# A two-layer trunk on one core: gate projections moved beside the block inverses, background blocks held back during one, and their weights loaded one call ahead

## The chip, the cores and the metric

The kernel runs on one core of a Trainium2 chip. The metric is the device time of one execution in microseconds (us). Each kernel is run several times and the median counts. One further execution is profiled; all durations below come from it.

The core has a matrix engine (PE, with its weight loads shown apart as PEld), a vector engine (DVE), an activation engine (ACT), a general engine (POOL) and a queue engine (SP) that issues most DMA transfers. Each engine takes its instructions strictly in the order of the program, and waits with everything behind it when one is not ready.

## The reference

A trunk of two layers over 1024 tokens of 1024 features. Layer 0 mixes the tokens by a gated delta net, layer 1 by retention; both are followed by a convolutional feed-forward network. Six vectors per layer (shift, scale and gate of mixer and network) come from a conditioning vector `e` and a large matrix `ada_w`. Cut to what matters here:

```python
def gated_deltanet(h, w_in, conv_w, a_log, dt_bias, norm_w, w_out):   # 8 heads of 128, chunks of 64
    qkv, z, a, bt = jnp.split(h @ w_in, ...)
    qkv = jax.nn.silu(causal_dwconv(qkv, conv_w))
    ...
    sol = lax.linalg.triangular_solve(kk + eye, rhs, left_side=True, lower=True, unit_diagonal=True)
    ...
    _, o = lax.scan(step, state0, xs)
    o = o * lax.rsqrt(jnp.mean(o * o, axis=-1, keepdims=True) + 1e-6) * norm_w
    o = o * jax.nn.silu(z)
    return o.reshape(...) @ w_out

def reference(...):
    e = jax.nn.silu(c @ cond_w + cond_b)
    for i in range(DEPTH):
        mod = (e @ ada_w[i] + ada_b[i])[:, None, :]
        sh1, sc1, g1, sh2, sc2, g2 = jnp.split(mod, 6, axis=-1)
        y = mixers[i % N_MIXERS](x * (1.0 + sc1) + sh1)
        x = layer_norm(DN_ALPHA * x + (1.0 + g1) * y, ln_g[i, 0], ln_b[i, 0])
        y = conv_ffn(x * (1.0 + sc2) + sh2, ...)
        x = layer_norm(DN_ALPHA * x + (1.0 + g2) * y, ln_g[i, 1], ln_b[i, 1])
```

## The kernel before

**Arithmetic.** All products are single precision, made of three products of a high and a low part each (`mm3`: low by high, high by low, high by high). A weight block of 128x1024 is loaded into a buffer `wr` (`load_w`, L102), ACT copies it to the high part `wh` (L89) and DVE subtracts to get the low part `wl` (L90). `wr`, `wh` and `wl` have two buffers each: a load starts when the split of the block two before has ended. All these loads are issued by SP, in program order.

**The delta-net phase** (about 87 to 658 us of the span) is written as streams: Python generators that issue instructions and name the next time on a hand-kept clock (`run`, table `LAT`) at which they want to go on. `run` always takes the stream that is ready and has the lowest number. The order that PE gets in this phase is pinned to the order of issue (`pq`, under L636 and L639); the other engines' orders are made by a list scheduler, which may move an instruction ahead of others of its engine. The streams are:

- `filler`: the projections, as items. An item "c" is one block of 128 features of q, k or v for all tokens: 48 matmuls of 128x512, then the causal convolution (`conv_half`), eight rows of DVE at L457. An item "z" is one block of the gate projection (weights `gdn_wz`): 48 matmuls as well, then SiLU on ACT (L1084) and a store to scratch memory `zd` (L1085). The items in the list `items` are all "c"; a "z" is put in by `filler` where a "c" would wait for a `qkv` buffer, and the rest of the eight at the end.
- `t_front(p)`: decays and key products of a pair of heads.
- `t_solve(0)` and `t_solve(1)`: for four heads each, the inverses of all 32x32 triangular blocks by forward substitution on DVE: a transpose X to Y (L797), 31 steps of a multiply (L805) and a subtract (L807), and transposes RX (L811) and TX (L815) of the result; ACT copies between them.
- `t_chain(p)`: builds the inverses of 64x64 and 128x128 from these on PE, beginning with 64 matmuls of 32x32.
- `prep(p)`, `dt_half(p, h)` (DT, L953), `scan(p, half)` (u, L976; Sn, L989) and a tail: products for the scan, the scan over chunks and its normalisation.

After the phase, `gate_phase` reads the gates back from `zd` (zg, L1116), multiplies them with the normalised output (L1129), and the output projection with `gdn_wout` (L303 to L305) follows, first for one half of the tokens, then for the other.

**Background blocks.** The vectors that are needed later are made in small units: `bg_ada` appends to the list `bg` eight units for each vector. A unit loads 512 KB of `ada_w` into a `wr` buffer (tile `mvw`, L210) and adds two rows of blocks to an accumulator on DVE (L214, L216); the last unit of each half also uses PE and ACT (L226 to L230). `filler` runs one unit after every item (`bg_step`), so a unit's load is issued right before the rows that use it. Three vectors (24 units) are made in this phase. Other units run in the feed-forward and retention phases, from `strassen` and other places, there with tiles of the tag `lane` where `bg_tag` says so.

**At the start** the first half's transposed input blocks 0 to 3 are held in two tiles of the tag `xT`, blocks 4 to 7 in `wr` buffers (`hold`).

## Time and profile before

| what | value |
|---|---|
| median of 3 runs | 3033.51 us (3031.15 to 3038.18) |
| the profiled execution | 3032.61 us, of which its span 3030.8 us |
| mean granted PE clock | 0.971 |
| memory traffic | 450.22 MB, mean 149 GB/s |
| weight loads for the feed-forward network | 96 of 512 KB, landing 4.0 us after issue (median) |
| loads of `ada_w` | 80 of 512 KB |

The span is the time from the first to the last recorded instruction; the execution's own time is 1.8 us longer. A row of a groups view reads: line, engine, operation, output<-input by the program's names, shape, count, then busy us, mean ns of one, idle time of the engine just before, and what ended most of it. A timeline row begins with the start and the duration in us. A row of waits gives engine, tile and line, the engine waited for with its tile and line, and us, times, longest.

The page's picture of the whole span, in 40 slices of about 76 us with the busy share in tenths:

```profile
PE   8889998999999999998999999999999899999997
DVE  5785786545888888998788645566688887778988
ACT  4655555434544445445432442222243544445442
```

The delta-net phase is the second to the ninth digit of a row. The prediction shows the further lines.

### The profile page before, as it was taken

How to read it: one execution, taken by the hardware profiler on the slowest of the kernel's cores; microseconds unless marked ns; L12 is line 12 of the kernel's file. 1: busy time of each engine (PE TensorE's matmuls, PEld its weight loads, DVE VectorE, ACT ScalarE, POOL GpSimd, SP SyncE). 2: the span in 40 equal slices, each digit the busy share in tenths (PEclk: the TensorE clock that was granted, in tenths of full speed). 3: DMA queues.
4: the chain of work that ended last, by engine and by line, in shares of the span. 5: the costliest groups of instructions: out<-in, count | busy, mean ns of one | idle time of the engine just before them, and what ended most of it. 6: DMA issues, size and time to landing. Idle time of an engine off the chain costs nothing. (4 is left out here: it accounts for less than half of the span.)

```text
span 3030.8 us, 38796 instructions
## 1 busy us (share of the span) xinstructions
PE 2840.2 (94%) x13590; PEld 2312.4 (76%) x13590; DVE 2271.4 (75%) x3841; ACT 1316.8 (43%) x2408; POOL 672.8 (22%) x629
## 2 busy tenths in 40 slices
PE   8889998999999999998999999999999899999997
PEld 7768876887778788786777787767777678888785
DVE  5785786545888888998788645566688887778988
ACT  4655555434544445445432442222243544445442
POOL 0410311033021111730023303422200011113704
PEclk9999998999999999999999999999998999999998
DMA  7222221354344545854322444666663332336663
GB/s 271 89 70 74 98 82 62 116 170 138 106 153 151 158 158 182 309 193 141 126 105 98 166 160 144 200 184 186 202 217 132 98 136 104 105 105 227 232 188 108
DMA packets 243027, 450.22 MB, mean 149 GB/s; under 512 B 22928, under 2 KB 76432, under 8 KB 242832
## 3 DMA queue, kind: packets, MB, share of 16 engines
q1 hardware_dynamic: 211648, 400.02, 40.0%
q10 hardware_dynamic: 29760, 43.00, 3.9%
q0 software_dynamic: 1424, 4.72, 0.4%
q8 instruction: 107, 1.75, 0.2%
q14 instruction: 88, 0.72, 0.1%
HBM read 339.13 MB, written 108.53 MB: 148 GB/s over the span
## 5 line engine op out<-in xcount | busy, mean ns | idle before, releaser
L636 PE MATMUL acc<-hT,wh 128*128 128x512 f32 x960 | 302.8, 397 | 0.0
L1556 POOL TENSOR_TENSOR o<-o 128x512 f32<-128x512 f32 x88 | 121.1, 1386 | 725.4 <-DVE o L1549 622.9
L279 PE MATMUL acc<-bb,ab 128*128 128x512 f32 x504 | 205.5, 408 | 18.8 <-DVE bb L90 18.7
L1158 PE MATMUL acc<-T,wb 128*128 128x512 f32 x840 | 205.3, 393 | 8.7 <-DVE wb L90 8.6
L636 PEld LDWEIGHTS acc<-hT,wh 128*128 128x128 f32 x960 | 184.3, 192 | 34.5
L278 PE MATMUL acc<-bb,ab 128*128 128x512 f32 x504 | 192.2, 407 | 16.9 <-DVE ab L90 10.3
L636 PE MATMUL acc<-hT,wl 128*128 128x512 f32 x480 | 204.3, 426 | 0.3 <-ACT sg L1084 0.3
L89 ACT ACTIVATE ab<-ar 128x512 fp32r<-128x512 f32 x210 | 129.8, 624 | 168.6 <-PE acc L280 87.9
L280 PE MATMUL acc<-bb,ab 128*128 128x512 f32 x504 | 202.6, 403 | 0.0
L1158 PEld LDWEIGHTS acc<-T,wb 128*128 128x128 f32 x840 | 157.9, 189 | 46.1 <-DVE wb L90 12.4
L90 DVE TENSOR_TENSOR wb<-wr,wb 128x512 fp32r<-128x512 f32 x162 | 116.0, 718 | 92.8 <-ACT wb L89 89.5
L90 DVE TENSOR_TENSOR ab<-ar,ab 128x512 fp32r<-128x512 f32 x210 | 169.2, 812 | 15.1 <-ACT ab L89 14.7
L90 DVE TENSOR_TENSOR wl<-wr,wh 128x1024 fp32r<-128x1024 f32 x85 | 106.4, 1252 | 89.7 <-ACT wh L89 89.7
L90 DVE TENSOR_TENSOR wb<-mm,wb 128x512 fp32r<-128x512 f32 x216 | 145.1, 683 | 22.8 <-ACT wb L89 20.9
L89 ACT ACTIVATE wh<-wr 128x1024 fp32r<-128x1024 f32 x101 | 106.8, 1058 | 121.3 <-PE acc L636 56.1
L89 ACT ACTIVATE wb<-mm 128x512 fp32r<-128x512 f32 x216 | 122.8, 593 | 72.5 <-DVE mm L1204 72.4
L1215 ACT ACTIVATE pc<-acc 128x512 f32<-128x512 f32 x143 | 84.5, 593 | 154.0 <-PE acc L1158 95.2
L636 PE MATMUL acc<-wh,hT 128*128 128x512 f32 x384 | 138.0, 422 | 2.0 <-DVE vv L90 2.0
L89 ACT ACTIVATE wb<-wr 128x512 fp32r<-128x512 f32 x162 | 99.3, 627 | 92.2 <-DMA wr<-in_ffn_up 45.9
L1535 DVE SCALAR_TENSOR_TENSOR o<-g,vc,o 128x512 f32<-128x512 f32 (+2 forms) x176 | 138.2, 804 | 0.8 <-ACT o L1530 0.2
L457 DVE SCALAR_TENSOR_TENSOR qkv<-raw,vc,qkv 128x512 f32<-128x512 f32 x144 | 114.6, 800 | 30.4 <-ACT qkv L455 29.3
L279 PEld LDWEIGHTS acc<-bb,ab 128*128 128x128 f32 x504 | 98.9, 196 | 44.7 <-DVE bb L90 24.3
(634 smaller groups left out, 7792.0 us busy)
## 6 DMA issues: line engine op xcount, KB each, us to landing
wr<-in_ffn_up SPq DMA_DIRECT2D x96, 512.0 KB, 4.0
mvw<-in_ada_w SPq DMA_DIRECT2D x80, 512.0 KB, 4.3
ad<-o SPq DMA_DIRECT2D x154, 256.0 KB, 2.2
ar<-ad SPq DMA_DIRECT2D x154, 256.0 KB, 4.4
Br<-in_ffn_down SPq DMA_DIRECT2D x88, 256.0 KB, 4.1
wr<-in_ret_wv SPq DMA_DIRECT2D x32, 512.0 KB, 3.7
ar<-od SPq DMA_DIRECT2D x56, 256.0 KB, 5.3
xs<-xt ACTq DMA_DIRECT2D x24, 512.0 KB, 3.8
```

The lines of the kernel that those rows point to most:

```text
L89: act.activation(dst_h, src, AF.Copy)
L90: eng.tensor_tensor(dst_l, src, dst_h, ALU.subtract)
L278: mm(acc, a[1][:, sl], w[0], start=first, stop=False)
L279: mm(acc, a[0][:, sl], w[1], start=False, stop=False)
L280: mm(acc, a[0][:, sl], w[0], start=False, stop=last)
L457: dve.scalar_tensor_tensor(oh, raw[:, 3 - j:515 - j], w[:, 3 - j:4 - j], oh, ALU.mult, ALU.add)
L636: pq(pe.matmul(out, lhsT, rhs, start=start, stop=stop), cost)
L1158: return pe.matmul(*a, skip_group_check=True, **kw)
L1215: act.activation(t, X, AF.Copy)
L1535: dve.scalar_tensor_tensor(tv, gv[:, c0 - j:c1 - j], w[:, 2 - j:3 - j], tv, ALU.mult, ALU.add)
L1556: pool.tensor_tensor(o[d], o[x], o[y], op)
```

## The change

It has five parts.

1. The order of the items is fixed. z 0, 1 and 2 follow the item (c, 0), in the place where solve 0 runs; z 3 follows the last k item (c, K + 7); z 4 to 7 come at the end. Before, `filler` placed the first two at a later point and six at the end.
2. A flag `quiet` is set when `t_solve` takes its tile X and cleared when it has issued TX; `filler` runs no background unit while it is set.
3. A background entry is now a pair of a fetch and a unit. `bg_step` issues the fetch of the next entry before it runs the current unit; `bg_flush`, at the start and the end of `strassen`, runs a unit whose fetch is out without fetching a further one.
4. `wr` has three buffers. For it the tag `xT` goes: blocks 0 to 3 of the first half are held in tiles of the tag `cv`.
5. The three vectors of this phase are made in the order 2, 4, 3, not 4, 3, 2.

The diff, shortened:

```diff
...
     dr = ctx.enter_context(tc.tile_pool(name="dr", bufs=1, space=bass.MemoryType.DRAM))
 
     BUFS = {"hTa": 8, "hTb": 8, "qkv": 24, "aux": 4, "auh": 8, "lane": 4, "cv": 4, "ada": 1,
-            "wr": 2, "wh": 2, "wl": 2, "t2": 3, "sm": 14, "sm2": 6, "st": 8, "s8": 6, "S": 4, "qx": 3, "fs": 1, "xT": 2}
+            "wr": 3, "wh": 2, "wl": 2, "t2": 3, "sm": 14, "sm2": 6, "st": 8, "s8": 6, "S": 4, "qx": 3, "fs": 1}
 
     def tl(tag, shape, dt=F32, name=None):
         return sb.tile(shape, dt, tag=tag, name=name or tag, bufs=BUFS[tag])
...
     bg_ps = [None]
     bg_tag = ["wr"]
 
-    def bg_step(tile=mm_tile):
+    def bg_step(tile=mm_tile, ahead=True):
         bg_ps[0] = tile
         if bg:
-            bg.pop(0)()
+            unit = bg.pop(0)[1]
+            if ahead and bg and bg[0][0]:
+                bg[0][0]()
+                bg_ahead[0] = True
+            else:
+                bg_ahead[0] = False
+            unit()
+
+    bg_ahead = [False]
+
+    def bg_flush():
+        if bg_ahead[0]:
+            bg_step(ahead=False)
 
     def gemm_feat(src, hT_, step=True):
         w = load_w(src)
...
     def bg_ada(i, j, kind):
         box = {}
 
+        def fetch(nh, kp):
+            wr = box[nh, kp] = tl(bg_tag[0], [P, 2, HALF], name="mvw")
+            c0 = j * D + nh * HALF
+            sp.dma_start(wr, A["ada_w"][i, kp * 256:(kp + 1) * 256, c0:c0 + HALF].rearrange("(a p) n -> p a n", p=P))
+
         def unit(nh, kp):
             if kp == 0:
                 box["a"] = tl("ada", [P, HALF])
             a = box["a"]
-            wr = tl(bg_tag[0], [P, 2, HALF], name="mvw")
-            c0 = j * D + nh * HALF
-            sp.dma_start(wr, A["ada_w"][i, kp * 256:(kp + 1) * 256, c0:c0 + HALF].rearrange("(a p) n -> p a n", p=P))
+            if (nh, kp) not in box:
+                fetch(nh, kp)
+            wr = box.pop((nh, kp))
             for kk in range(2):
                 k = kp * 2 + kk
                 if k == 0:
...
 
         for nh in range(2):
             for kp in range(KT // 2):
-                bg.append(lambda nh=nh, kp=kp: unit(nh, kp))
+                bg.append((lambda nh=nh, kp=kp: fetch(nh, kp), lambda nh=nh, kp=kp: unit(nh, kp)))
 
     def fold(i, which, ln_idx):
         sh, sc = vecs[i, 3 * which], vecs[i, 1 + 3 * which]
...
 
         for c in range(2):
             for r in range(8):
-                bg.append(lambda c=c, r=r: unit(c, r))
+                bg.append((None, lambda c=c, r=r: unit(c, r)))
 
     def ln_hooks(half, xts, tag, vecs2, out, dst, key, npool=0):
         def build(f):
...
                     xT["w"] = tl("wr", [P, 2, HALF], name="xT")
                 t = xT["w"][:, f % 2]
             else:
-                t = tl("auh" if half else "xT", [P, HALF], name="xT")
+                t = tl("auh", [P, HALF], name="xT") if half else tl("cv", [P, 516], name="xT")[:, 0:HALF]
             act.activation(t, turn(half, f), AF.Copy)
             xT[half, f] = t
 
...
         yield after_ev(("T0", 2 * qd_ - 1), ("A", 2 * qd_), ("A", 2 * qd_ + 1))
         yield from take("lane", 1)
         X = tl("lane", [P, 32, 32], name="X")
+        quiet[0] = True
         for h in pairs[2 * qd_] + pairs[2 * qd_ + 1]:
             for b in range(4):
                 bs = slice(32 * b, 32 * b + 32)
...
         TX = tl("lane", [P, 32, 32], name="TX")
         dve.transpose(flat(TX), flat(TP))
         RTX[qd_] = (RX, TX)
+        quiet[0] = False
         give("lane", 1)
         emit(("Tq", qd_))
         emit(("T", qd_), LAT["T"])
...
             give("lane", 1)
             emit(("M", p))
 
-    bg_ada(0, 4, "col")
-    bg_ada(0, 3, "col")
-    bg_ada(0, 2, "col")
+    for j in (2, 4, 3):
+        bg_ada(0, j, "col")
     kept = {}
     zd = dr.tile([GH, P, S], F32, tag="zd", name="zd")
 
...
         ssq_tile(ti, ptr)
         emit(("f", ti), 1.0)
 
+    quiet = [False]
+
     def filler(items):
-        spare = [(z, k) for k in range(GH)]
-        todo = list(items)
-        while todo or spare:
-            if not todo or (todo[0][0] == "c" and free["qkv"] < 2 and len(spare) > 4):
-                kind, ti = spare.pop(0)
-            else:
-                kind, ti = todo.pop(0)
+        for kind, ti in items:
             if kind == "h":
                 if ti > 1:
                     acc = acc_tile()
...
                     yield [(0.2, ssq_late(ti))]
                 else:
                     emit(("f", ti), LAT["fv"])
-            bg_step(acc_tile)
+            if not quiet[0]:
+                bg_step(acc_tile)
 
     LAT = {"kk": 3.05, "ld": 1.14, "g1": 17.30, "gm": 2.50, "mm": 1.81, "T": 4.98, "X": 3.38, "fs": 1.9, "T0": 5.00, "t1": 1.65, "t2": 2.35, "t3": 1.34, "D": 2.67, "s1": 1.60, "s2": 1.22, "s3": 1.26, "tail": 12.31, "ssq": 9.30, "fv": 2.85}
     pairs = [(2 * p, 2 * p + 1) for p in range(GH // 2)]
...
     events["Sh", -1] = events["Sh", -2] = 0.0
     c, z = "c", "z"
     K, V = GH, 2 * GH
-    items = [("h", 1), ("h", 2), ("h", 3), (c, K + 3), (c, V), (c, V + 1), (c, 0), (c, 1), (c, V + 2), (c, V + 3), (c, 2), (c, 3),
-             (c, K + 4), (c, K + 5), (c, K + 6), (c, K + 7), (c, V + 4), (c, V + 5), (c, 4), (c, 5), (c, V + 6), (c, V + 7), (c, 6), (c, 7)]
+    items = ([("h", 1), ("h", 2), ("h", 3), (c, K + 3), (c, V), (c, V + 1), (c, 0), (z, 0), (z, 1), (z, 2)]
+             + [(c, k) for k in (1, V + 2, V + 3, 2, 3, K + 4, K + 5, K + 6, K + 7)]
+             + [(z, 3), (c, V + 4), (c, V + 5), (c, 4), (c, 5), (c, V + 6), (c, V + 7), (c, 6), (c, 7), (z, 4), (z, 5), (z, 6), (z, 7)])
     todo = [(-1.0, gates()), (9.0, filler(items))]
     todo += [(0.3, t_solve(0)), (2.3, t_solve(1))]
     for p in range(4):
...
         return b
 
     def strassen(hT0, xts, scale, shift, items, tags=("hTb", "hTb", "qkv", "qkv", "aux"), direct=False):
+        bg_flush()
         B = {"11": hT0[:4], "21": hT0[4:]}
         nblk = [0]
         nacc = [0]
...
             wino(n, items[n][2]())
             if items[n][3]:
                 items[n][3]()
+        bg_flush()
         bg_tag[0] = "wr"
         return B
 
```

What moves on the engines, at three places. Line numbers of the changed kernel are up to 19 higher than those before: L805 and L807 (the solve's steps) are L823 and L825, L457 (convolution) is L474, L216 (background) is L233, L210 (its load) is L219.

DVE, in the middle of solve 0, before the change (fs and T are the solve's own, the number of elements rising and falling with the step):

```order
L805 TENSOR_TENSOR fs_1464<-Y_1459,T_1461 128x240
L457 SCALAR_TENSOR_TENSOR qkv_1658<-raw_1659,vc_153,qkv_1658 128x512
L807 TENSOR_TENSOR T_1461<-T_1461,fs_1464 128x20x12
L457 SCALAR_TENSOR_TENSOR qkv_1658<-raw_1659,vc_153,qkv_1658 128x512
L90 TENSOR_TENSOR wl_1772<-wr_1769,wh_1771 128x1024
L805 TENSOR_TENSOR fs_1464<-Y_1459,T_1461 128x247
L457 SCALAR_TENSOR_TENSOR qkv_1658<-raw_1659,vc_153,qkv_1658 128x512
L807 TENSOR_TENSOR T_1461<-T_1461,fs_1464 128x19x13
L457 SCALAR_TENSOR_TENSOR qkv_1714<-raw_1715,vc_153,qkv_1714 128x512
L805 TENSOR_TENSOR fs_1464<-Y_1459,T_1461 128x252
L457 SCALAR_TENSOR_TENSOR qkv_1714<-raw_1715,vc_153,qkv_1714 128x512
```

The same stretch of the changed kernel:

```order
L90 TENSOR_TENSOR wl_1621<-wr_1618,wh_1620 128x1024
L825 TENSOR_TENSOR T_1463<-T_1463,fs_1466 128x23x9
L823 TENSOR_TENSOR fs_1466<-Y_1461,T_1463 128x220
L825 TENSOR_TENSOR T_1463<-T_1463,fs_1466 128x22x10
L823 TENSOR_TENSOR fs_1466<-Y_1461,T_1463 128x231
L825 TENSOR_TENSOR T_1463<-T_1463,fs_1466 128x21x11
L823 TENSOR_TENSOR fs_1466<-Y_1461,T_1463 128x240
L233 SCALAR_TENSOR_TENSOR ada_1900<-mvw_2158,e_162,ada_1900 128x512
L825 TENSOR_TENSOR T_1463<-T_1463,fs_1466 128x20x12
L233 SCALAR_TENSOR_TENSOR ada_1900<-mvw_2158,e_162,ada_1900 128x512
L823 TENSOR_TENSOR fs_1466<-Y_1461,T_1463 128x247
```

The convolutions are gone from between the steps; the weight split (L90) stays, and two background rows stand in a place where before there were none.

SP, where it issues the loads for the items around solve 0, before the change (wr is a weight block of an item, mvw a background block, Ld and DT belong to the decays):

```order
L102 DMA wr_1671<-in_gdn_wqkv 128x1024
L210 DMA mvw_1765<-in_ada_w 128x2x512
L102 DMA wr_1769<-in_gdn_wqkv 128x1024
L210 DMA mvw_2062<-in_ada_w 128x2x512
L102 DMA wr_2077<-in_gdn_wqkv 128x1024
L210 DMA mvw_2276<-in_ada_w 128x2x512
L102 DMA wr_2280<-in_gdn_wz 128x1024
L945 DMA DT_1800<-Ld_734 128x512 x2
L210 DMA mvw_2492<-in_ada_w 128x2x512
L102 DMA wr_2496<-in_gdn_wz 128x1024
```

and after it:

```order
L102 DMA wr_1536<-in_gdn_wz 128x1024
L774 DMA Ld_734<-U_889 128x1024
L774 DMA Ld_734<-U_1084 128x1024
L102 DMA wr_1618<-in_gdn_wz 128x1024
L102 DMA wr_1700<-in_gdn_wqkv 128x1024
L219 DMA mvw_1898<-in_ada_w 128x2x512
L102 DMA wr_1903<-in_gdn_wqkv 128x1024
L219 DMA mvw_2158<-in_ada_w 128x2x512
L102 DMA wr_2162<-in_gdn_wqkv 128x1024
L219 DMA mvw_2313<-in_ada_w 128x2x512
```

Three gate blocks now come ahead of the q, k, v blocks, with no background load between them, and the background loads resume behind the item after the last gate block, where solve 0 has not ended.

DVE, at the end of solve 1, before the change (RX and TX are the last transposes of the solve):

```order
L805 TENSOR_TENSOR fs_3914<-Y_3909,T_3911 128x31
L807 TENSOR_TENSOR T_3911<-T_3911,fs_3914 128x31
L811 STREAM_TRANSPOSE RX_4212<-T_3911 128x1024
L216 SCALAR_TENSOR_TENSOR ada_4640<-mvw_4833,e_162,ada_4640 128x512
L815 STREAM_TRANSPOSE TX_4216<-TP_4214 128x1024
L216 SCALAR_TENSOR_TENSOR ada_4640<-mvw_4833,e_162,ada_4640 128x512
L953 TENSOR_TENSOR DT_4218<-DT_4218,mm_4237 128x512
L953 TENSOR_TENSOR DT_4218<-DT_4218,mm_4338 128x512
L953 TENSOR_TENSOR DT_4222<-DT_4222,mm_4344 128x512
```

and after it:

```order
L474 SCALAR_TENSOR_TENSOR qkv_4354<-raw_4355,vc_153,qkv_4354 128x512
L823 TENSOR_TENSOR fs_3956<-Y_3951,T_3953 128x87
L825 TENSOR_TENSOR T_3953<-T_3953,fs_3956 128x3x29
L823 TENSOR_TENSOR fs_3956<-Y_3951,T_3953 128x60
L825 TENSOR_TENSOR T_3953<-T_3953,fs_3956 128x2x30
L823 TENSOR_TENSOR fs_3956<-Y_3951,T_3953 128x31
L825 TENSOR_TENSOR T_3953<-T_3953,fs_3956 128x31
L829 STREAM_TRANSPOSE RX_4232<-T_3953 128x1024
L833 STREAM_TRANSPOSE TX_4236<-TP_4234 128x1024
L972 TENSOR_TENSOR DT_4238<-DT_4238,mm_4333 128x512
```

Background rows no longer stand among the last rows of this solve; convolutions and a split of the items beside it do.

## Prediction

> **What bounds the kernel now.** The page's span and busy times come first.
>
> ```profile
> span 3030.8 us, 38796 instructions
> PE 2840.2 (94%) x13590; PEld 2312.4 (76%) x13590; DVE 2271.4 (75%) x3841; ACT 1316.8 (43%) x2408; POOL 672.8 (22%) x629
> ```
>
> PE works 2840.2 of 3030.8 us, and the change takes no matmul away. At most the 190.6 us in which PE stands idle, and what a slow clock costs, can be won. So I read next what PE waits for (waits view: engine, tile and line, awaited engine, us, times, longest).
>
> ```profile
> PE mm L636 <- DVE DT L953: 19.9, 2, 11.1
> PE acc L279 <- DVE bb L90: 18.7, 9, 4.0
> PE sc L1158 <- DVE wb L90: 14.5, 5, 5.2
> ```
>
> The largest entry is two waits only. PE's timeline (start, duration, group, idle time before it) places them.
>
> ```profile
> 223.35 2.08 PE L636 MATMUL mm<-qkv 128*128 128x128 f32 x8 [11.09 <-DVE DT L953]
> ...
> 226.96 0.62 PE L636 MATMUL acc<-hT,wh 128*128 128x512 f32 x2
> ...
> 231.72 2.08 PE L636 MATMUL mm<-T,U 32*32 32x32 f32 x64 [0.77 <-DVE qkv L918]
> ...
> 473.63 2.07 PE L636 MATMUL mm<-qkv 128*128 128x128 f32 x8 [8.80 <-DVE DT L953]
> ...
> 477.77 3.43 PE L636 MATMUL mm<-T,U 32*32 32x32 f32 x64
> ...
> 483.01 1.05 PE L636 MATMUL acc<-hT,wh 128*128 128x512 f32 x2
> ...
> 487.83 0.62 PE L636 MATMUL acc<-hT,wh 128*128 128x512 f32 x2
> 488.29 0.40 PE L636 MATMUL acc<-hT,wl 128*128 128x512 f32 x1
> ...
> 488.99 0.39 PE L636 MATMUL acc<-hT,wl 128*128 128x512 f32 x1
> ```
>
> The 64 matmuls of 32x32 (231.72, 477.77) open the chains that need a solve's result. Shortly before each, PE has run out of work for 11.09 and 8.80 us: DVE is still solving, and the DVE rows that PE names stand behind the solve in DVE's queue. After the second gap a pair of wide matmuls takes 1.05 us where it takes 0.62 later, so PE is also slow there for about 12 us (473.6 to some 485.6), about 5 us lost; after the first gap it is back at 0.62 by 226.96, a loss of about 1.5 us. At full speed the three products of a block start 0.70 us apart (488.29, 488.99), 0.23 us for a wide matmul.
>
> Now what DVE does from Y to TX of each solve (groups view, windows 171.69 to 220.93 and 419.33 to 471.88: busy us, mean ns, idle before and its releaser).
>
> ```profile
> L457 DVE SCALAR_TENSOR_TENSOR qkv<-raw,vc,qkv 128x512 f32<-128x512 f32 x18 | 13.4, 746 | 0.1
> L807 DVE TENSOR_TENSOR T<-T,fs 128x31 f32<-128x31 f32 (+15 forms) x31 | 10.6, 341 | 0.7
> L805 DVE TENSOR_TENSOR fs<-Y,T 128x31 f32<-128x31 f32 (+15 forms) x31 | 10.5, 339 | 0.6
> L216 DVE SCALAR_TENSOR_TENSOR ada<-mvw,e,ada 128x512 f32<-128x512 f32 x5 | 3.7, 742 | 2.0 <-DMA mvw<-in_ada_w 2.0
> L90 DVE TENSOR_TENSOR wl<-wr,wh 128x1024 fp32r<-128x1024 f32 x3 | 3.6, 1217 | 0.0
> L918 DVE TENSOR_TENSOR qkv<-mm,ir 128x512 f32<-128x512 f32 x4 | 2.7, 687 | 0.1
> ...
> L457 DVE SCALAR_TENSOR_TENSOR qkv<-raw,vc,qkv 128x512 f32<-128x512 f32 x22 | 16.4, 744 | 0.3 <-ACT qkv L455 0.2
> L216 DVE SCALAR_TENSOR_TENSOR ada<-mvw,e,ada 128x512 f32<-128x512 f32 x10 | 7.4, 744 | 1.4 <-DMA mvw<-in_ada_w 1.4
> L90 DVE TENSOR_TENSOR wl<-wr,wh 128x1024 fp32r<-128x1024 f32 x3 | 3.7, 1217 | 0.0
> L918 DVE TENSOR_TENSOR qkv<-mm,ir 128x512 f32<-128x512 f32 x3 | 2.1, 684 | 0.0
> ```
>
> Of 49.2 us the 62 solve steps need 21.1; the largest guest is the convolution of the qkv items, 13.4 us. Busy times overlap slightly: all groups of the first window add up to some 49.1 us of busy and 4.7 us of idle in 49.2 us, so a row is worth about 0.91 of its busy time (0.89 in the second window, by the same count).
>
> **Solve 0: the main term.** By the new order no L457 row stands between Y and TX, because three z items fill PE there and give DVE only their weight split: -13.4 x 0.91 = -12.2 us. Two scaling rows fewer (L918): -1.2. The background rows do not go: there are 6 where there were 5, +0.7. "No background beside a solve" is set when the units are issued, but the rows of two units issued later, or earlier, still stand between the steps. Each of their three loads can start only when the split just ahead of it has freed a buffer, and is used some six steps (2.5 us) later.
>
> ```profile
> mvw<-in_ada_w SPq DMA_DIRECT2D x80, 512.0 KB, 4.3
> ...
> DVE ada L216 <- DMA mvw<-in_ada_w: 26.8, 17, 5.5
> ```
>
> A load lands 4.3 us after issue (median) and one wait has lasted 5.5 us. I take 4.3 - 2.5 = 1.8, with the issue about 2 us for each of the three: 6.0 where the window now has 2.0, +4.0 (ends: -2.0 if all land in time, 3 x 5.5 - 2.0 = +14.5 if each is as late as the longest). DVE's sum is -12.2 - 1.2 + 0.7 + 4.0 = -8.7 us. ACT then copies the results out.
>
> ```profile
> 219.68 1.25 DVE L815 STREAM_TRANSPOSE TX<-TP 128x1024 f32<-128x1024 f32 x1 [0.75 <-ACT TP L813]
> ...
> 224.72 4.06 ACT L842 ACTIVATE T<-TX 32x256 f32<-32x256 f32 x6
> ```
>
> TX ends at 220.9, the copies at 228.8, 7.9 us later. With TX at 212.2 the copies end at 220.1 and the chain starts about 220.7, not 231.7: **-11.0 us**, if PE gets there. The windows view (length, then busy PE, PEld, DVE, ACT, POOL, granted clock, DMA share, GB/s) bounds that.
>
> ```profile
> 164.60:212.30 47.70, 44.50 (x220) 36.42 (x218) 43.90 (x94) 22.99 (x61) 4.20 (x9) 1.00 0.29 89
> 223.30:231.70 8.40, 7.60 (x40) 6.40 (x41) 4.16 (x7) 7.65 (x20) 1.66 (x7) 0.82 0.00 0
> ```
>
> Ahead of the chain PE has 44.5 + 7.6 = 52.1 us of work from 164.6, less 1.5 for the slow clock: it can be there at 215.2 and no sooner. (The new order puts more wide matmuls and fewer transposes ahead of it, about the same time.) So the ends are -16.5 us (PE bound) and about 0 (the long load waits).
>
> **Solve 1.** Here the background rows do leave: 11 rows (10 of L216, one L214) of 7.9 us busy, -7.0, and their 1.4 us of wait. Two convolutions, one split and one scaling row come in: +1.3 +1.1 +0.6. DVE is 5.4 us shorter. But rows near the solve's end wait for transposes that stand behind some 15 more wide matmuls (15 x 0.23 = 3.5 us), and DVE takes rows in order. I take **-3.5 us**, ends 0 and -8.8.
>
> A rule bears on what a shorter gap is worth. The Trainium skill, TensorE: Matmul & The Clock Gate, Part 1: The HAM clock gate, states that an idle window of about 3.4 us halves PE's clock and a busy one of about 3.4 us restores it. The first gap agrees (full speed 3.6 us after it), the second does not (12 us). By it my two remaining gaps of about 5 us would still be followed by the slow clock, as the sum has it; only a gap under 3.4 us would win the 5 us more, which is in the third rival.
>
> **Scans 0 and 1** lose two z items as filler and get qkv items: 2 x 8 convolutions, 16 x 0.746 x 0.9 = 10.7 us more on DVE.
>
> ```profile
> 300.00:340.00 40.00, 39.64 (x289) 35.63 (x287) 24.94 (x56) 20.64 (x41) 13.52 (x16) 1.00 0.24 86
> 520.00:560.00 40.00, 37.09 (x401) 32.52 (x400) 22.62 (x59) 19.16 (x52) 4.90 (x10) 0.96 0.08 28
> ```
>
> DVE is busy 24.9 of 40 us in such a stretch, so it has room; PE's idle time is 0.4 of 40 us beside one kind of filler and 2.9 beside the other. Over 108 us (231.7 to 340) the ends are 0 and 2.7 x 2.5 = +7; I take the low side, near the first row, **+1.5**.
>
> **The end of the phase.** Four z items remain behind the last solve, not six, so the last scan has less cover.
>
> ```profile
> 631.12 0.38 PE L636 MATMUL acc<-w,DT 128*128 128x128 f32 x2
> ...
> 657.85 0.48 PE L303 MATMUL acc<-wh,hl 128*128 128x512 f32 x1
> ...
> 644.32 0.60 PE L639 MATMUL mm<-cst,qkv 128*128 128x128 f32 x4
> ...
> 636.32 1.78 DVE L1016 TENSOR_TENSOR qkv<-qkv,so 128x512 f32<-128x512 f32 x1
> ...
> 652.39 0.69 DVE L1129 TENSOR_TENSOR ot<-ot,zg 128x512 f32<-128x512 f32 x1 [10.20 <-DMA zg<-zd]
> ```
>
> Between the last scan matmul and the output projection lie 26.7 us of z matmuls. Two items are 96 matmuls, 22.1 us at 0.23: 4.6 stay. The last normalised output is ready 7.0 us after that matmul (638.1), but the projection begins with the other half of the sequence. If all of the 7.0 is needed, 2.4 us come out; with the transposes of that output, which PE starts at 644.32, it would be 13.2 - 4.6 = 8.6. I take **+1.0**, ends 0 and +8.6.
>
> **The rest.** At the start a 512 KB load now goes ahead of four loads of x on SP: **+0.5**, ends 0 and one landing, 4.3. The third buffer also serves every weight stream later; DVE waits there for weights, but short.
>
> ```profile
> DVE mm L1204 <- DMA wr<-in_ffn_up: 34.8, 29, 2.4
> ```
>
> 29 waits of 1.2 us, on an engine that PE in turn waits for 14.5 us in one place: **-1.0**, ends -8 (half of that) and +3 (loads ahead that delay others). Which of the three background vectors comes first costs nothing: none is used before the phase ends.
>
> **Sum:** -11.0 - 3.5 + 1.5 + 1.0 + 0.5 - 1.0 = -12.5 us. The profiled execution took 3032.6 us, 0.9 below the median shown of 3033.5, so 3020.1 against the one and 3021.0 against the other; I say 3020.5.
>
> **Rivals.** (1) *The stall only moves.* The three loads hold DVE in solve 0 for 10 to 15 us instead of 6, so its term is -7 to -2, PE waits at the chain for the loads in place of the convolutions, and solve 1 gives nothing; with the other terms' +2.0 that is 3027.6 to 3032.6. For it: the order keeps these rows and their loads start late. Against it: 12.2 us of convolutions do go. (2) *Slower: the scans become bound by DVE.* Each scan step passes DVE twice (u and Sn), each time behind a convolution of 0.67 us now; two pairs of 8 steps: 32 x 0.67 = 21 us. It decides as soon as PE's fixed order leaves a step's two DVE rows less time than one convolution more. Then 3032.6 - 12.5 + 20 = 3040. Against it: the stretch 520 to 560 has qkv filler and only 2.9 us idle. (3) *More than that:* both gaps vanish (-11.1 - 8.8) with the slow stretches (-1.5 - 5), and the other terms stay at +2.0: 3008; with the weight streams at -8 in place of -1, 3001. It needs the three loads to land in time and DVE's rows at the end of solve 1 not to wait for PE. For it: PE could be at the first chain at 215.2. Against it: ACT's 7.9 us of copies stand between TX and each chain, and the change leaves them.
>
> **Chances.** Forecast, 3013 to 3026: 0.50. Rival 1: 0.21, three quarters of it within 6 us of no change. Rival 2: 0.11. Rival 3: 0.18. By a bound of 0.2%, 6 us, which is what a measurement of this kernel can tell from no change: faster 0.50 + 0.18 + 0.05 = 0.73, same 0.16, slower 0.11. The range, 3002 to 3036, takes in nearly all of rival 3 and leaves out most of rival 2.
>
> **What would show it.** Right: no L457 rows between Y and TX of solve 0, that window at about 40 us, the first 32x32 group some 11 us earlier, PE's wait for DT at 8 to 12 us in place of 19.9; four z items at the end with no PE gap over 2 us at the output projection. Wrong: waits for mvw of over 3 us inside solve 0 (rival 1); PE idle of over 5 us between 230 and 340, named u or Sn (rival 2); pairs of wide matmuls at 0.62 right behind both chains (rival 3).

## The result, and the profile after

The changed kernel took 3060.64 us (median of 4 runs, 3053.14 to 3061.22); the kernel before, measured again beside it, 3035.85 us (median of 4). The ratio is 1.0079, with a 95% interval of 1.0052 to 1.0105: **slower**, by 0.8% or about 24 us, which is clear of the noise. The prediction said 3020.5 and ended its range at 3036. Line numbers of the kernel after are about 17 to 19 higher: L636 is now L653, L639 is L656, L815 is L833, L303 is L320.

The first lines of the page of the kernel after:

```profile
span 3059.2 us, 38806 instructions
...
PE 2862.6 (94%) x13590; PEld 2317.9 (76%) x13590; DVE 2292.7 (75%) x3841; ACT 1320.0 (43%) x2410; POOL 682.4 (22%) x629
```

The span grew by 28.4 us. PE's idle time grew by only 6.0 us (3059.2 - 2862.6 = 196.6, before 190.6); its busy time grew by 22.4 us, with the same 13590 matmuls. The mean granted clock is the same, 0.972 after and 0.971 before. The prediction looked for everything in the idle time and in what a slow clock costs. So there are two things to find: why the same matmuls take longer, and why the idle time did not shrink.

What PE waits for, in the kernel after (waits view: engine, tile and line, awaited engine, us, times, longest):

```profile
PE mm L653 <- ACT T L861: 15.4, 4, 11.3
...
PE mm L656 <- DVE qkv L1035: 6.0, 1, 6.0
```

The wait for DT, 19.9 us before, has fallen to 3.3 us. In its place stand a wait for the copies that end a solve (ACT T) and a new wait of 6.0 us for L1035, the last row of a scan's tail.

DVE inside solve 0 of the kernel after, first the two transposes that bound it (timeline: start, duration, group, idle before it), then the groups between them (busy us, mean ns, idle before):

```profile
174.69 1.25 DVE L815 STREAM_TRANSPOSE Y<-X 128x1024 f32<-128x1024 f32 x1 [1.09 <-ACT X L811]
...
212.60 1.25 DVE L833 STREAM_TRANSPOSE TX<-TP 128x1024 f32<-128x1024 f32 x1 [0.96 <-ACT TP L831]
```

```profile
L825 DVE TENSOR_TENSOR T<-T,fs 128x31 f32<-128x31 f32 (+15 forms) x31 | 10.6, 342 | 0.8
...
L233 DVE SCALAR_TENSOR_TENSOR ada<-mvw,e,ada 128x512 f32<-128x512 f32 x6 | 4.5, 750 | 2.8 <-DMA mvw<-in_ada_w 2.8
L90 DVE TENSOR_TENSOR wl<-wr,wh 128x1024 fp32r<-128x1024 f32 x3 | 3.7, 1218 | 0.0
```

The solve takes 39.2 us, from 174.69 to 213.85, where it took 49.2. No convolution is among its groups, six background rows are, and they wait 2.8 us for their loads. This is the picture that the prediction drew. (The solve also begins 3.0 us later than before, at 174.69 and not at 171.69.) PE's timeline of the kernel after, at the first two chains and at the chain behind solve 1, shows what came of it:

```profile
219.51 1.06 PE L653 MATMUL mm<-T,U 32*32 32x32 f32 x16 [2.29 <-ACT T L861]
221.45 2.57 PE L653 MATMUL mm<-T,U 32*32 32x32 f32 x48 [0.88 <-ACT T L861]
...
224.54 1.06 PE L653 MATMUL acc<-hT,wh 128*128 128x512 f32 x2
...
285.19 2.11 PE L653 MATMUL mm<-T,U 32*32 32x32 f32 x64
...
488.05 1.06 PE L653 MATMUL mm<-T,U 32*32 32x32 f32 x16 [11.32 <-ACT T L861]
```

The first chain starts at 219.5 instead of 231.7, 12.2 us sooner, and the gap is down to 2.29 us. But the second chain starts at 285.19 (before: 287.6). Of the 12.2 us, 2.4 are left. A pair of wide matmuls takes 1.06 us at 224.54 where it takes 0.62 at full speed. And the gap at solve 1 is not smaller but larger: 11.32 us against 8.80. The windows view (length, then busy PE, PEld, DVE, ACT, POOL, granted clock, DMA share, GB/s) of the 17.1 us at the first chain, after and then before:

```profile
219.70:236.80 17.10, 16.22 (x182) 13.12 (x180) 6.16 (x14) 7.49 (x12) 0.12 (x1) 0.51 0.10 32
```

```profile
231.70:248.80 17.10, 16.94 (x264) 14.51 (x265) 11.79 (x28) 9.64 (x15) 0.55 (x2) 1.00 0.28 95
```

Before, the clock was full through the chain. After, it was at half through 17.1 us in which PE was busy for 16.2. Before, 10.2 us at half clock lay ahead of the chain, from 216.1 to 226.3, and PE was busy in only 3.0 us of them: most of the slow time fell into the gap.

The time until the feed-forward network starts was 812.1 us before and is 825.3 us after, as the trace's first feed-forward matmul has it, first before, then after:

```profile
812.14 0.39 PE L110 MATMUL sc<-hT,wb 128*128 128x512 f32 x1
```

```profile
825.34 0.39 PE L110 MATMUL sc<-hT,wb 128*128 128x512 f32 x1
```

So 13 of the 28 us of span are lost by the end of the part that the change reorders, and 15 behind it, where the new order of items has no part, but the third buffer, the loads ahead and the places of the tiles do.

### The profile page after: what moved, and what is told of

It reads as the page before. It is cut to its first block, busy times and chain, and to the rows that moved or that the text cites. A ratio compares the mean times of both kernels' runs of the same rounds, so it can differ in the third digit from the quotient of the medians.

```text
span 3059.2 us, 38806 instructions
## 1 busy us (share of the span) xinstructions
PE 2862.6 (94%) x13590; PEld 2317.9 (76%) x13590; DVE 2292.7 (75%) x3841; ACT 1320.0 (43%) x2410; POOL 682.4 (22%) x629
## 5 line engine op out<-in xcount | busy, mean ns | idle before, releaser
L653 PE MATMUL acc<-hT,wh 128*128 128x512 f32 x960 | 304.8, 399 | 0.0
L653 PEld LDWEIGHTS acc<-hT,wh 128*128 128x128 f32 x960 | 185.6, 193 | 34.9
L653 PE MATMUL acc<-hT,wl 128*128 128x512 f32 x480 | 206.1, 429 | 0.0
L89 ACT ACTIVATE ab<-ar 128x512 fp32r<-128x512 f32 x210 | 129.1, 622 | 114.7 <-PE acc L297 49.0
L90 DVE TENSOR_TENSOR wl<-wr,wh 128x1024 fp32r<-128x1024 f32 x85 | 108.6, 1278 | 92.9 <-ACT wh L89 86.2
L90 DVE TENSOR_TENSOR ab<-ar,ab 128x512 fp32r<-128x512 f32 x210 | 161.8, 780 | 18.8 <-ACT ab L89 18.7
L90 DVE TENSOR_TENSOR wb<-mm,wb 128x512 fp32r<-128x512 f32 x216 | 145.5, 684 | 26.0 <-ACT wb L89 24.8
L89 ACT ACTIVATE wh<-wr 128x1024 fp32r<-128x1024 f32 x101 | 106.7, 1058 | 113.5 <-PE acc L653 67.6
L89 ACT ACTIVATE wb<-mm 128x512 fp32r<-128x512 f32 x216 | 123.4, 595 | 69.8 <-DVE mm L1221 63.1
L653 PE MATMUL acc<-wh,hT 128*128 128x512 f32 x384 | 137.7, 421 | 2.6 <-DVE mv L1769 1.7
L474 DVE SCALAR_TENSOR_TENSOR qkv<-raw,vc,qkv 128x512 f32<-128x512 f32 x144 | 114.0, 793 | 31.2 <-ACT qkv L472 30.1
L89 ACT ACTIVATE wb<-wr 128x512 fp32r<-128x512 f32 x162 | 101.3, 626 | 82.3 <-PE acc L1175 52.5
L90 DVE TENSOR_TENSOR bb<-Bw,bb 128x512 fp32r<-128x512 f32 x120 | 124.5, 1048 | 13.4 <-ACT bb L89 13.4
L90 DVE TENSOR_TENSOR wb<-wr,wb 128x512 fp32r<-128x512 f32 x162 | 117.0, 724 | 20.4 <-ACT wb L89 19.2
```

Source lines behind the costliest of these rows:

```text
L89: act.activation(dst_h, src, AF.Copy)
L90: eng.tensor_tensor(dst_l, src, dst_h, ALU.subtract)
L474: dve.scalar_tensor_tensor(oh, raw[:, 3 - j:515 - j], w[:, 3 - j:4 - j], oh, ALU.mult, ALU.add)
L653: pq(pe.matmul(out, lhsT, rhs, start=start, stop=stop), cost)
```

## The experiments

All times are medians. Ratios are to the kernel before, measured in the same batch on the same chip, with 95% intervals; "+10 us" is a ratio times 3035 us. "3-1-4" is short for the order after: three z items beside solve 0, one at solve 1, four at the end. What follows is sorted by question, not by the order of the runs.

### Where the tiles lie

In the changed kernel `hold` uses the tag `cv` at the start, and the tag `xT` is gone. In this program a tag gets its place in the on-chip memory (SBUF) at its first use, as the addresses of the two kernels show. So the four `cv` tiles, 8320 bytes in each partition (16 x 512 + 128), now lie ahead of the tags `aux`, `wr`, `qkv` and `auh`, which all move by an odd 128 bytes. The program's addresses, joined with the trace, say how long a wide matmul takes from start to start (after 660 us, steps under 300 ns; each operand's address modulo 512, count, mean ns; the last column also has a few with other offsets):

```
                       both at 32        one at 160, the other at 32   all wide matmuls
before                 8397   227.3      -                             8514   226.64
after                  5376   228.1      3045   232.9                  8543   229.15
```

The theory: a matmul whose stationary and moving operands start at different offsets modulo 512 bytes is slower. Four kernels test it. The first puts an unused tile of 384 bytes behind the first `cv` tile in the kernel after, which brings all back to 32. The others only shift the kernel before: one set of tags by 128 bytes, as the change did; all tiles to 0; all tiles to 160.

```diff
 e1_pad384 (after), in hold:
+            if "pad" not in xT:
+                xT["pad"] = sb.tile([P, 96], F32, tag="pad", name="pad", bufs=1)
 e2_before_pad128 (before), in hold:
+        if "pad" not in xT:
+            xT["pad"] = sb.tile([P, 32], F32, tag="pad", name="pad", bufs=1)
 e3_before_front480 (before), ahead of all tiles:
+    ct("pad", [P, 120])
 e4_before_front128 (before), ahead of all tiles:
+    ct("pad", [P, 32])
```

> The changed kernel with one unused tile of 384 bytes per partition behind the first tile of the tag cv, so that every wide tile behind it starts at 32 modulo 512 bytes again, as before the change; nothing else. Theory A (placement: a 128x512 matmul is slower where an operand does not start at 32 modulo 512): PE's busy time falls from 2862.6 to about 2840, the start-to-start time of wide matmuls from 229 to 230 ns back to 227, and the time from 3060.6 to about 3038. Theory B (the third buffer and the earlier loads disturb PE's reads): no change, 3055 to 3061.

> The kernel before with one unused tile of 128 bytes behind the first tiles of wl, so that the tiles behind it start at 160 modulo 512; no other part of the change. Theory A: PE's busy time rises from 2840 to about 2860 and the time from 3036 to 3053 to 3060. Theory B: no change, 3031 to 3040.

> The kernel before with 480 unused bytes ahead of everything, so that all wide tiles start at 0 modulo 512. If an absolute alignment counts (theory A1), this is at least as good as 32: 3036, or clearly faster when 227 ns at 32 still holds a penalty. If only the place of one operand against the other counts (A2), exactly as before: 3031 to 3040. Theory B: no change.

> The kernel before with 128 unused bytes ahead of everything, so that all wide tiles start at 160 modulo 512. A1 (absolute alignment): every wide matmul is at 229 to 238 ns, PE's busy time rises by 30 to 60 us, 3065 to 3095. A2 (only the place of one operand against the other): no change, 3031 to 3040. Theory B: no change.

| kernel | us | ratio | all wide matmuls, start to start |
|---|---|---|---|
| e1, after with the pad | 3044.43 | 1.0020 (1.0004 to 1.0037) | 226.6 ns |
| e2, before, some tags +128 | 3046.97 | 1.0034 (1.0019 to 1.0050) | 229.2 ns |
| e3, before, all at 0 | 3030.50 | 0.9978 (0.9966 to 0.9991) | 226.7 ns |
| e4, before, all at 160 | 3034.21 | 0.9994 (0.9982 to 1.0007) | 226.7 ns |

Where both operands lie alike, the mean is 227.3 ns in e1 (both at 32) and e3 (both at 0) and 227.4 in e4 (both at 160). In e2 it is 233.0 ns where one lies at 160 and the other at 32, whichever of the two it is.

Late in the program PE is busy all the time, so the windows view of 2600 to 2700 us can be read as a count: so many matmuls in 100 us. Before, after, e2 and e1:

```profile
2600.00:2700.00 100.00, 100.00 (x443) 82.84 (x442) 75.25 (x113) 48.77 (x82) 14.15 (x10) 1.00 0.30 100
```

```profile
2600.00:2700.00 100.00, 100.00 (x437) 81.81 (x436) 72.24 (x109) 45.26 (x77) 11.17 (x8) 1.00 0.29 93
```

```profile
2600.00:2700.00 100.00, 100.00 (x437) 81.74 (x436) 72.08 (x108) 44.43 (x76) 16.74 (x12) 1.00 0.32 110
```

```profile
2600.00:2700.00 100.00, 100.00 (x443) 82.84 (x442) 73.64 (x110) 45.13 (x78) 16.77 (x12) 1.00 0.33 113
```

At a full clock, 443 matmuls before and with the pad, 437 after and in e2: 1.4% slower there. The groups view of 2500 to 2800 us, by form, tells which matmuls pay; first the kernel before, then after:

```profile
L1158 PE MATMUL acc<-T,wb 128*128 128x512 f32 x240 | 57.6, 389 | 0.0
...
L111 PE MATMUL acc<-hT,wb 128*128 128x512 f32 x79 | 30.7, 389 | 0.0
```

```profile
L1175 PE MATMUL acc<-T,wb 128*128 128x512 f32 x252 | 61.8, 394 | 0.0
L111 PE MATMUL acc<-hT,wb 128*128 128x512 f32 x84 | 32.8, 390 | 0.0
```

With the tile T, which has moved, the mean goes from 389 to 394 ns; with hT, whose tag kept its place, from 389 to 390. Undoing the shift in the kernel after wins 16 us by the medians (3060.6 to 3044.4) and 18 by the ratios, and making it in the kernel before costs 10 us. Moving all tiles together costs nothing (e3, e4): it is the offset between the two operands that counts, not the offset itself. Only a shift of 128 bytes between them was tested, so that 512 is the right number to divide by is not shown, and no run tells why the pair is slower. By the spacing one would expect 8543 x 2.5 ns = 21 us; e1 and e2 lie below that, and runs differ in their time at half clock, so I take placement as 10 to 18 us. Why e3 is 0.2% faster than before at an unchanged spacing stays open. The Trainium skill, SBUF — State Buffer, Operand start alignment, asks only that an operand start at a multiple of its element size, and says that this is about legality, not speed. Offsets 32 and 160 both meet that, and the runs show that a pair of them is slower than a pair of equal ones.

### The order of the items

With the placement repaired, 6 us of loss are left. Two kernels separate the order of the items from the rest of the change: the kernel before with the new list alone, and the padded kernel after with the old way of choosing.

```diff
 e5_items_only (before):
-        while todo or spare:
...
+        for kind, ti in items:
...
+    items = ([("h", 1), ("h", 2), ("h", 3), (c, K + 3), (c, V), (c, V + 1), (c, 0), (z, 0), (z, 1), (z, 2)]
+             + [(c, k) for k in (1, V + 2, V + 3, 2, 3, K + 4, K + 5, K + 6, K + 7)]
+             + [(z, 3), (c, V + 4), (c, V + 5), (c, 4), (c, 5), (c, V + 6), (c, V + 7), (c, 6), (c, 7), (z, 4), (z, 5), (z, 6), (z, 7)])
 e6_pad_olditems (after with the pad): the same lines the other way round
```

> The kernel before with the new order of items alone (z 0 to 2 beside solve 0, z 3 ahead of solve 1, four z at the end); no quiet flag, no load ahead, two wr buffers, old placement of tiles. Theory C (what is left of the loss once the placement is put right comes from this order: slow clock in the first chain +10, solve 1 +5, end of the phase +9 to 10, against -10 at solve 0): 3040 to 3048, and the start of the feed-forward network 10 us or more later than before. Theory D (it comes from the earlier loads, the third buffer or the quiet flag): 3020 to 3036.

> The padded changed kernel with the old way of choosing items: quiet flag, load ahead, third buffer, the order of the background vectors, not the new order of items. Theory C: no loss, 3028 to 3038. Theory D: 3042 to 3048.

e5 took 3055.20 us, 1.0055 (1.0034 to 1.0077): the new order alone costs 17 us. e6 took 3027.24 us, 0.9973 (0.9957 to 0.9989): the rest alone gains 8. Together that is +9, near the +6 of e1, so the two parts about add up. (e5 lies 7 us above the range given for theory C, so the order costs more than was thought.) PE's timeline at the output projection says where the order loses. First the kernel after, then e5:

```profile
656.41 0.50 PE L320 MATMUL acc<-wh,hl 128*128 128x512 f32 x1 [0.83 <-DVE hl L90]
...
664.59 0.50 PE L320 MATMUL acc<-wh,hl 128*128 128x512 f32 x1 [1.50 <-ACT sg L1098]
...
673.13 1.09 PE L656 MATMUL mm<-cst,qkv 128*128 128x128 f32 x4 [5.95 <-DVE qkv L1035]
```

```profile
656.39 0.50 PE L303 MATMUL acc<-wh,hl 128*128 128x512 f32 x1 [1.47 <-DVE hl L90]
...
664.59 0.50 PE L303 MATMUL acc<-wh,hl 128*128 128x512 f32 x1 [1.52 <-ACT sg L1078]
...
673.10 1.09 PE L639 MATMUL mm<-cst,qkv 128*128 128x128 f32 x4 [5.92 <-DVE qkv L1016]
```

The two agree within 0.03 us at 664.59 and 673.1, though one has the old placement and background. The z matmuls run out during the last scan, the output projection of the other half begins, and then PE's fixed order holds it for the transposes of the last tail, which wait for that tail's last row. The clock has dropped as well: four transposes take 1.09 us where they took 0.60 before.

How much this costs can be read in all the profiles, as the time from the first matmul of the output projection to the first of the feed-forward network. It is 168 to 169 us in the four kernels that have four z items at the end (after, e1, e5, e8) and 154 to 157 in the twelve that have five or six; before, it is 154.3. Up to the output projection the new order is no loss: its start comes 1.5 us sooner in e5 than before, and 5.5 us sooner in e1 than in e6.

Two kernels then change only the number of z items by place.

```diff
 e7_pad_2z6z (after with the pad): 2-0-6, in the same way
 e13_305 (after with the pad): 3-0-5
-             + [(z, 3), (c, V + 4), ...
+             + [(c, V + 4), (c, V + 5), (c, 4), (c, 5), (c, V + 6), (c, V + 7), (c, 6), (c, 7), (z, 3), (z, 4), (z, 5), (z, 6), (z, 7)])
```

> The padded changed kernel with two z items beside solve 0, none at solve 1, and six at the end as before. If four z at the end are too few to cover the last scan (part of theory C), the stretch from the output projection to the feed-forward network returns to about 154 us from 168, and the time falls by 8 to 10 us from 3044, to 3034 to 3037; if the end costs nothing, no change.

> The padded changed kernel with three z items beside solve 0, none ahead of solve 1 and five at the end, without unused matmuls. If the slow clock of the first chain alone makes the difference to the same order with 14 unused matmuls (3021): 3026 to 3031, the first chain to the second about 66 us. If the end and solve 1 make all the loss of the items: 3019 to 3024, and the first chain costs nothing in the sum.

e7 took 3025.40 us, 0.9964 (0.9948 to 0.9979), and e13 3022.09 us, 0.9958 (0.9941 to 0.9974). The timeline of e13 at the same place:

```profile
656.32 0.61 PE L655 MATMUL acc<-hT,wh 128*128 128x512 f32 x2
656.78 1.05 PE L1594 MATMUL mm<-dg,ones 128*128 128x128 f32 x8
657.58 0.48 PE L320 MATMUL acc<-wh,hl 128*128 128x512 f32 x1
```

With five z items at the end PE passes from z to the output projection with no gap. One item moved is worth 19 us between e1 and e13 (1.0020 to 0.9958), about the whole cost of the new order (14 to 17). In the two profiles 13.5 us of it are there when the feed-forward network starts (826.7 and 813.2 us), nearly all won behind the start of the output projection. The rest comes later, where PE worked 101 us at half clock in e1's profile and 80 in e13's; why is open. e7 came out 9 us below the range that it was given. Against e6, e13 is 0.15% lower, well inside the intervals: that three z items beside solve 0 gain anything over the old way is not shown.

### The half clock at the chains

The third theory: the 17 us at half clock behind a shorter gap eat what the gap gave. The test keeps PE busy with unused wide matmuls ahead of the first and the third chain, so that the clock stays up; e10 and e9 do so in two other orders.

```diff
 e8_pad_warm (after with the pad), in t_chain:
+        if p % 2 == 0:
+            wt = acc_tile()
+            for _ in range(48 if p else 14):
+                pm(wt, hT[0][0][0][:, 0:P], hT[0][0][0], cost=0.0)
 e9_215_warm: order 2-1-5, and the 48 alone
 e10_305_warm: order 3-0-5, and the 14 alone
```

> The padded changed kernel with unused wide matmuls issued on PE right ahead of the first 32x32 matmuls of each solve's first chain: 14 (3.2 us) at the first, 48 (11 us) at the second; nothing reads them. Theory E (the gap ahead of a chain of small matmuls leaves the clock halved for 17 us of real work, which gives back what the shorter gap won): the first chain to the second takes about 56 us in place of 66, the same after the second solve, and the time falls by 10 to 16 us, to 3028 to 3035. Rival F (these stretches are long because the chains wait for other engines): no change or up to 5 us slower.

> The padded changed kernel with two z items beside solve 0, one ahead of solve 1 and five at the end, and 48 unused wide matmuls ahead of the first chain of solve 1 (none at solve 0). If the end of the phase is covered by five z and the clock theory (E) holds at solve 1: below both the run with two and six (3025) and the run with unused matmuls alone (3022), 3012 to 3020. If the end needs six z, or if the gain of the unused matmuls came from the first chain alone: 3022 to 3032.

> The padded changed kernel with three z items beside solve 0, none ahead of solve 1, five at the end, and 14 unused wide matmuls ahead of the first chain of solve 0 only. Theory E at the first chain alone, with the end covered: 3014 to 3024, the first chain to the second in about 56 to 60 us. If the gain of the unused matmuls came from solve 1: 3025 to 3035.

e8 took 3021.58 us, 0.9953 (0.9933 to 0.9974); e9 3022.42, 0.9967 (0.9948 to 0.9986); e10 3021.13, 0.9949 (0.9927 to 0.9971). The windows row of e8 at the first chain, and its wait at the output projection:

```profile
219.00:236.10 17.10, 15.51 (x228) 12.57 (x227) 6.86 (x15) 9.70 (x16) 0.56 (x2) 0.90 0.10 33
```

```profile
673.67 1.09 PE L658 MATMUL mm<-cst,qkv 128*128 128x128 f32 x4 [7.03 <-DVE qkv L1041]
```

The clock at the chain is 0.90, as meant, where it is 0.50 in e1, and the stretch from the first to the second chain shrinks from 65.8 us (e1) to 60.5; theory E had about 56. But e13, which has the same order there and no unused matmuls, takes 61.6 us, with the clock at 0.80:

```profile
220.80:237.90 17.10, 15.12 (x220) 12.86 (x221) 6.53 (x15) 9.21 (x15) 0.87 (x4) 0.80 0.11 33
```

So the half clock of 17 us behind the first chain does not come every time, and how much of the 5 us is due to the unused matmuls is not shown. Both kernels still need some 5 us more than the 55.9 of the kernel before, with 4 us of idle time of PE in the stretch where there was 1: the slow clock is only a part of what eats the gain. In e8 PE then waits 7.03 us for the same last tail, and the feed-forward network starts at 825.3 us against 826.7 in e1. In the profiles the gain at the chains is gone before the phase ends. e8's median is still 23 us under e1's, below the range of theory E. In the profiles that comes after this point, where PE worked 75 us at half clock in e8's profile and 101 in e1's; whether the unused matmuls have anything to do with that is open. With five z at the end they win nothing that can be told (e10 against e13: 0.9949 and 0.9958).

### Loads ahead, and the quiet flag

Three kernels take the other two parts of the change apart: loads ahead with the third buffer, in the old order and without the flag; the flag alone in the kernel before, with the order 2, 4, 3; and 2-0-6 without the flag.

```diff
 e11_ahead_only (e6, without the flag) and e14_206_noquiet (e7, without the flag):
-        quiet[0] = True
 e12_quiet_only (before):
+        quiet[0] = True
...
+        quiet[0] = False
...
+            if not quiet[0]:
+                bg_step(acc_tile)
```

> The padded kernel with the old items and without the quiet flag: load ahead, third wr buffer, the order of the background vectors. Theory G (the loads ahead and the third buffer bring the gain of 8 to 9 us of all parts but the items): 3024 to 3030. Theory H (the quiet flag brings it): 3033 to 3038.

> The kernel before with the quiet flag and the order 2, 4, 3 of the background vectors alone; two wr buffers, no load ahead, old items, old placement. Theory G: no change, 3032 to 3040. Theory H: 3024 to 3031.

> The padded kernel with two z items beside solve 0 and six at the end, load ahead and third buffer, without the quiet flag. If the flag costs 2 to 4 us even with the loads ahead: 3018 to 3024, the best of all. If the flag is worth its name beside this order: 3026 to 3032.

e11 took 3024.05 us, 0.9965 (0.9949 to 0.9980): loads ahead and the third buffer gain 11 us without the other two parts. No run tells the loads ahead from the third buffer. e12 took 3047.56, 1.0047 (1.0029 to 1.0066): the flag without loads ahead costs 14, outside the ranges of both theories. With loads ahead the flag makes no difference that can be told: e6 against e11 (0.9973, 0.9965), and e7 against e14, which took 3021.07, 0.9959 (0.9942 to 0.9977). Why the flag alone costs 14 us was not followed further; in the profiles 10 us of it are lost before the output projection starts (668.0 us against 657.9).

The 11 us of e11 are won behind the phase. Its feed-forward network starts 5 us later than before, but from there to the end it takes 2199 us where the kernel before takes 2219; half of the 19 us is less idle time of PE, the other half less work at half clock. The shorter waits for loads show in the waits view of the kernel after:

```profile
DVE mm L1221 <- DMA wr<-in_ffn_up: 21.1, 27, 2.2
DVE ada L233 <- DMA mvw<-in_ada_w: 13.2, 15, 1.4
```

Before, DVE waited 34.8 us for the first of these, and in ACT's list stood a further 45.9 us for the same weights (wb, L89), which has no row any more. DVE's wait for `ada_w` at this line (L216 then) was 26.8 us.

### The whole difference

| part | alone, on the kernel before | in the kernel after, by undoing it |
|---|---|---|
| placement of the tiles | +10 (e2) | +18 (after against e1) |
| order of the items | +17 (e5) | +14 (e6 against e1) |
| loads ahead, third buffer | -11 (e11, padded) | |
| quiet flag | +14 (e12) | +2, not told from 0 (e6 against e11) |

An entry of the left column has an interval of 5 to 7 us to either side; those of the right column are differences of two ratios and have 7 to 10. The right column with the -11 makes +23, near the +24 measured, but that is no check: from before to e11, e6, e1 and after, each kernel is the one ahead of it with one part more, so the steps must add up. The left column does check it: +30 with the flag's 14, +18 with its 2, on either side of 24. Nine kernels are faster than before with an interval that leaves out 1 (e3, e6 to e11, e13 and e14), by 0.2 to 0.5%. Five of them, e8 to e10, e13 and e14, lie near 3021 or 3022 us. Of these e13 is nearest to the change: the change with the pad, and with z 3 at the end.

## Why the prediction was wrong

**"... the change takes no matmul away. At most the 190.6 us in which PE stands idle, and what a slow clock costs, can be won"**: this step failed first. It took PE's time for each matmul at a full clock as fixed, and the sum has no term for what the freed tag and the early use of `cv` do to the addresses. Measured: +10 (e2) to +18 us (after against e1). Nothing in the trace of before could have priced it, for there nearly all wide matmuls have operands that lie alike (8397 of 8514); but that tiles move by an odd 128 bytes can be read from the pool.

**The end of the phase, +1.0, ends 0 and +8.6**: the mechanism was seen, with the right rows, and its size was missed. The working had 2.4 us if the tail's last row is needed and 8.6 if its transposes are, and took less than half of the smaller one because the projection "begins with the other half". It does, but in PE's fixed order the last tail's transposes stand inside that half's projection, and everything behind them waits. The three gaps add 0.83 + 1.50 + 5.95 = 8.3 us, about the upper end, and the half clock behind them comes on top: from the output projection to the feed-forward network the kernel after takes 14.6 us longer than before (168.9 and 154.3).

**Solve 0, -11.0**: right, by the working given and some luck. The window is 39.2 us (said: about 40), the background rows stayed, six of them, and the chain starts 12.2 us sooner. The waits for `mvw` were 2.8 us, not 6.0, so rival 1 is out. The luck is that two misses cancel: TX ended at 213.85 us, 1.7 later than forecast, because the solve began 3.0 us later, and the chain began 5.7 us after TX and not 8.5.

**What that is worth**: wrong. The sum carried the 11 us through to the end; of 12.2 us at the first chain 2.4 are left at the second, and 1.5 at the output projection (656.4 and 657.9 us). In the kernel after the gap ahead of the chain was 2.29 us, and the clock was still at half for 17.1 us while PE was 95% busy. The Trainium skill, TensorE: Matmul & The Clock Gate, Part 1, has an idle window of about 3.4 us halve the clock and a busy one of about 3.4 us restore it. By the rule 3.4 us of work would have ended it; the runs disagree. The third rival's condition, a gap under 3.4 us, was met at the first solve, and its gain did not follow.

**Solve 1, -3.5, ends 0 and -8.8**: wrong in sign. The gap went from 8.80 to 11.32 us and now stands right ahead of the chain, for ACT's copies. DVE's window did shrink, from 52.5 to 49.9 us, but PE's work ahead of the chain now ends 11 us before the copies do. I counted DVE's rows and not PE's.

**Scans, +1.5**: small, as said. No wait of PE for u or Sn in the kernel after is over 1.5 us. PE's idle time between 230 and 340 us rose from 3.5 to 7.0, with 3.4 of it one wait for ACT (qkv, L475). So rival 2, slower by the scans, is not the reason, though the time came out on its side.

**The start and the rest, +0.5 and -1.0**: the rest was mis-sized. e11 puts it at -11 us, with the start in it, past the end of -8 that I gave. The start was not measured apart; solve 0 begins 3.0 us later. I had read DVE's wait for the weights and passed over the longer one in ACT's list.

So one gain was there to the end, some 11 us from the loads. The 12 us at solve 0 were lost again before the output projection, and two costs outweighed what was left: some 14 us at the end of the phase, and 10 to 18 us from the places of the tiles. The forecast took the first of them at less than a tenth and left the second out.

## What to carry to other kernels

After any change to a pool's tags or to the order of their first use, compare the tiles' addresses modulo 512 before reading the schedule: if the busy time of equal matmuls has grown at the same granted clock, it is not the schedule. Filler that is moved under one wait is taken from another; look in the engine's fixed order for what stands behind the last of it, and count that from its last dependency on. A gap that closes is worth its length only if the clock comes back in the work behind it.

## What the hardware showed

- A wide matmul (128x128 by 128x512, fp32r) starts 227.3 to 227.4 ns after the one before when both operands lie at the same offset modulo 512 bytes (32, 0 or 160 in before, e3 and e4), and 232.9 ns after it when one lies at 32 and the other at 160 (after).
- Half a clock can last long where the chains of 32x32 matmuls run: 17.1 us at 95% busy in the kernel after. It need not: in e13, with the same order there, it is 6.8 us, and in e8, with wide matmuls ahead, 3.4. In the delta-net phase the profiles show lengths from 3.4 to 20.5 us, all multiples of 3.4.
- PE works between 99 and 157 us of a run at half clock, by the 16 profiles, and loses about half of that (129 us before, 133 after). The mean clock differs from run to run of one kernel: e1's runs went from 3033 us at a mean clock of 0.975 to 3051 at 0.965. With this spread differences under 0.2% could not be told here.
